# Unnormalized keys and queries in a gated-delta-rule layer: where the norm factors are applied

## The chip, the cores and the metric

The kernel runs on one core of one Trainium2 chip. The metric is device time of one execution, in microseconds (us); lower is better. A core has five instruction streams: TensorE (PE in the profile, with its weight loads as PEld), VectorE (DVE), ScalarE (ACT), GpSimd (POOL) and SyncE (SP). Here SP issues nearly all DMA transfers, one after another in program order. An instruction that waits holds up all that stands behind it on its own stream.

## The reference

One transformer block on 256 tokens of width 2048, all in float32: a norm, an input projection, two mixers of eight heads each (a gated delta rule, "GDN", and a causal attention, "MOBA"), an output projection, and a mixture of 32 experts of width 512, two for each token. The change lies in the GDN heads:

```python
qh = l2norm(heads(q)) * (HEAD_DIM ** -0.5)      # x * rsqrt(sum(x*x) + 1e-6), per token and head
kh = l2norm(heads(k))
...
kb = k * beta[..., None]
L = jnp.where(strict, jnp.einsum('bhnid,bhnjd->bhnij', kb, k) * decay, 0.0)
rhs = jnp.concatenate([v * beta[..., None], kb * jnp.exp(g)[..., None]], axis=-1)
sol = lax.linalg.triangular_solve(eye + L, rhs, left_side=True, lower=True)
attn = jnp.where(causal, jnp.einsum('bhnid,bhnjd->bhnij', q, k) * decay, 0.0)
...
o = rmsnorm(o, out_norm_w) * jax.nn.silu(zf)
```

A norm factor is one number for each token and head, so it may be multiplied in before or after the products over the head dimension.

## The kernel before

**Projection stage.** The two projections are cut into 18 chunks of 512 output columns, and each chunk into 16 units of 128 rows of the weight, 288 units in all. The chunks come in this order (half 0 is heads 0 to 3, half 1 heads 4 to 7): gk0, gq0, gv0, gz0, mv0, gk1, gq1, gv1, mk0, mq0, mk1, gz1, mq1, mv1, wo0 to wo3. Chunk gz0 is thus units 48 to 63. A unit's float32 weight tile `w_raw` is loaded by SP, split by ACT into a rounded `w_hi` (line 210) and by DVE into the rest `w_lo` (line 213), and multiplied by PE in 12 matmuls (lines 232 to 236) or, in the gz, mv and wo chunks, in 6 of twice the width (lines 243 to 246), always into the tile `pj`. Loads are written up to eight units ahead (`RAWB = 4` tiles of two units), splits five units ahead of PE (`SPB = 6`).

**Tasks.** Everything else of the mixers is written as Python generators that a loop steps once for each unit (`tick`, at most three of them in a unit). The number that a `yield` gives is the wait in units, 2 if none. What a task issues in the step of unit n lies behind unit n's matmuls on PE, but behind the split of a later unit on ACT and DVE, and behind a later load on SP. This order is fixed when the program is built. A second list, `side`, is stepped twice in a unit and holds the triangular inverse (`inverse`), a long run of small DVE instructions.

**The GDN steps that the change touches**, for each half:

- `decay` loads, for each of four heads, rows of cumulated decay, broadcast over all partitions, from a DRAM tensor `drow` into a tile `E` (128x6x128): one load of slots 0 to 3 (line 396) and one of slots 4 and 5 (line 398), whose rows are those of slots 1 and 3 once more. Then POOL masks slots 0, 2, 4 and 5 (`affine_select`, line 405), and ACT takes exponentials of all six (lines 410 to 412).
- `qk_task` runs for k and then for q: a convolution and silu (`conv_silu`), squares, and column sums of the squares on PE (`pss`, line 463). After q, DVE adds epsilon (lines 469, 470), POOL raises 16 columns to the power -1/2 (`rk`, line 472), PE transposes them (`prk`, line 475), ACT copies them out (line 477), SP stores them to DRAM (line 480) and loads them broadcast as `RN`, 256 KB for each head (line 484), and POOL multiplies keys and queries by them (line 487, four `kq` multiplications of 128x512). Then for each head PE forms the products (`pA`, lines 493 and 498), DVE multiplies them by `E` (lines 495, 499), and SP stores part of `E` to DRAM as `dU` for the inverse.
- `v_task` transposes v (`pv`) and scales it by `beta` on its way out of PSUM (`bv`, line 570).
- `head_task` finishes the inverse, applies it, and forms the output `po`, its mean square (line 648), the root (lines 650, 651) and the gated output `og` (line 653).

PSUM tiles of all tasks come from one ring of four buffers (`ps_tmp`).

**Expert stage.** From unit 225 on, loads of expert weights are put between the loads of `w_out` into buffers that are free, and from the end of the projections on the kernel streams some 400 MB of expert weights through them (SP, line 940), each load waiting for PE to be done with a buffer.

Of the kernel before, what the change touches and what calls it, by code (L numbers as in the profile page):

```python
# [19 lines left out]
T = 256  # L20
# [27 lines left out]
def tile_block(ctx, tc, x, norm_mix_w, w_in, conv_w, A_log, dt_bias, gonw, monw, w_out, nfw,  # L48
# [28 lines left out]
    def ps_tmp(name):  # L77
        return pp.tile([128, 512], F32, name=name, tag="pt", bufs=4)
# [19 lines left out]
    nc.vector.memset(mhalf, -0.5)  # L98
    ones1 = prc.tile([128, 1], F32, name="ones1")
# [287 lines left out]
    E = {}  # L387

    def decay(hf):

        heads = range(4 * hf, 4 * hf + 4)
        for H in heads:
            e = wt("E", [128, 6, 128], "E", EB)
            E[H] = e
            off = drow.offset + H * 256
            nc.sync.dma_start(e[:, 0:4].rearrange("p (a b) t -> p a (b t)", a=2),
                              bass.AP(tensor=drow.tensor, offset=off, ap=[[0, 128], [2048, 2], [1, 256]]))
            nc.sync.dma_start(e[:, 4:6],
                              bass.AP(tensor=drow.tensor, offset=off + 128, ap=[[0, 128], [2048, 2], [1, 128]]))
            yield 1  # L400
        yield 1
        for H in heads:
            e = E[H]
            for s, op in ((0, OP.is_gt), (2, OP.is_ge), (4, OP.is_gt), (5, OP.is_ge)):
                nc.gpsimd.affine_select(out=e[:, s], in_=e[:, s], pattern=[[1, 128]], compare_op=op, fill=-BIG, base=0,
                                        channel_multiplier=-1)
            yield 1
        for H in heads:
            e = E[H]
            nc.scalar.activation(e[:, 0:4:2], e[:, 0:4:2], AF.Exp, bias=negG[:, 0, H:H + 1])  # L410
            nc.scalar.activation(e[:, 1:4:2], e[:, 1:4:2], AF.Exp, bias=suf[:, H:H + 1])
            nc.scalar.activation(e[:, 4:6], e[:, 4:6], AF.Exp, bias=negG[:, 1, H:H + 1])
            if H % 2:
                yield 1
# [24 lines left out]
    kq, bv, zs, pss, YY = {}, {}, {}, {}, {}  # L439

    def qk_task(hf, la, pb):
# [25 lines left out]
        rk = wt("rk", [128, 4, 2, 2], "rk", 1)  # L467
        psv = pss[hf][:, 0:16].rearrange("p (h a b) -> p h a b", h=4, a=2)
        nc.vector.tensor_scalar(rk[:, :, 0], psv[:, :, 0], EPS, None, op0=OP.add)
        nc.vector.tensor_scalar(rk[:, :, 1], psv[:, :, 1], EPS, float(HD), op0=OP.add, op1=OP.mult)  # L470
        rkf = rk.rearrange("p h a b -> p (h a b)")
        nc.gpsimd.tensor_tensor(rkf, rkf, mhalf, op=OP.pow)
        yield 4
        prk = ps_tmp("prk")
        nc.tensor.transpose(prk[:16, 0:128], rkf, ident)
        rks = wt("rks", [16, 128], "rks", 1)
        nc.scalar.copy(rks, prk[:16, 0:128])
        yield
        drk = drp.tile([16, 128], F32, name=f"drk{hf}")
        nc.sync.dma_start(drk, rks)  # L480
        yield
        RN = [wt("RN", [128, 2, T], "YY", 4) for _ in range(4)]
        for h in range(4):
            nc.sync.dma_start(RN[h].rearrange("p a t -> p (a t)"), bcast_rows(drk, h * 512, 512))
        yield
        for h in range(4):
            nc.gpsimd.tensor_mul(kq[4 * hf + h], kq[4 * hf + h], RN[h])
            yield 1
        for h in range(4):
            H = 4 * hf + h  # L490
            e = E[H]
            p0 = ps_tmp("pA0")
            nc.tensor.matmul(p0, kq[H][:, 0, 0:128], kq[H].rearrange("p a t -> p (a t)"), start=True, stop=True)
            e0 = e[:, 0:4].rearrange("p s t -> p (s t)")
            nc.vector.tensor_mul(e0, p0, e0)
            p1 = ps_tmp("pA1")
            p1v = p1[:, 0:256].rearrange("p (a t) -> p a t", a=2)
            nc.tensor.matmul(p1v, kq[H][:, 0, 128:256], kq[H][:, :, 128:256], start=True, stop=True)
            nc.vector.tensor_mul(e[:, 4:6], p1v, e[:, 4:6])
            yield 1  # L500
            nc.sync.dma_start(square(dU[hf], h), e[:, 0:5:4])
        yield
# [12 lines left out]
    def inverse(hf):  # L515
# [10 lines left out]
        for j in range(30, -1, -1):  # L526
            n = 32 - j
            pr = wt("ybp", [128, 8, 32], "ybp", 1)[:, :, 0:n]
            nc.vector.tensor_tensor(pr, UB[:, j, None, j:32].to_broadcast([128, 8, n]), YB[:, :, j:32], op=OP.mult)
            yield  # L530
            nc.vector.tensor_reduce(YB[:, :, j:j + 1], pr, axis=AX.X, op=OP.add, negate=True)
            yield
# [21 lines left out]
    def v_task(hf, pb):  # L554
# [7 lines left out]
        yield 1  # L562
        for h in range(4):
# [5 lines left out]
            for b in range(2):  # L569
                nc.scalar.activation(bv[H][:, b], pv[:, b * 128:(b + 1) * 128], AF.Copy, scale=beta[:, b, H:H + 1])  # L570
# [21 lines left out]
    def head_task(H):  # L592
# [53 lines left out]
        so = wt("so", [128, 2], "so", 6)  # L646
        for b in range(2):
            nc.scalar.activation(og[:, b], po[:, b * 128:(b + 1) * 128], AF.Square, accum_out=so[:, b:b + 1])
# [3 lines left out]
        yield 1  # L652
        for b in range(2):
# [804 lines left out]
```

## Time and profile before

| | |
|---|---|
| time, median of 3 runs (lowest to highest) | 1455.63 us (1455.09 to 1456.22) |
| the profiled execution: its time / its span | 1455.25 us / 1453.5 us |
| busy in the span: PE, DVE, ACT, POOL | 1392.8, 621.2, 414.4, 58.9 us |
| mean granted TensorE clock | 0.991 |
| bytes moved by DMA | 493.4 MB |

The span is from the first to the last instruction; 1.75 us of the time lie outside it. PE counts as busy nearly always, but its matmuls overlap, so a late operand shows partly as an idle gap and partly as a matmul that starts later than its predecessor would allow. In the projection stage the starts of units are therefore the better measure of pace. Starts are us from the span's start throughout.

### The profile page before, as it was taken

The numbers are of one execution on the slowest core, as the hardware profiler recorded it, in microseconds if no ns is written. First come the engines' busy times: TensorE is split into PE (matmuls) and PEld (weight loads), VectorE is DVE, ScalarE is ACT, GpSimd is POOL, SyncE is SP. The second block draws the span as 40 slices with busy tenths as digits, with TensorE's granted clock in tenths as the row PEclk, the third lists the DMA queues.
The fourth block names the chain that finished last, engine by engine and source line by source line (L and its number), as shares of the span: only waits on it lengthen the run. The fifth ranks groups of instructions, "written<-read, shape, count | busy, mean of one in ns | idle before, by whom it ended". The sixth has DMA issues, their size and how long they took to land.

```text
span 1453.5 us, 19069 instructions
## 1 busy us (share of the span) xinstructions
PE 1392.8 (96%) x7490; PEld 817.5 (56%) x7490; DVE 621.2 (43%) x1289; ACT 414.4 (29%) x803; POOL 58.9 (4%) x92
## 2 busy tenths in 40 slices
PE   8989999999999999999999999999999999899996
PEld 8976999898988853443443443443443344235332
DVE  6856977497665442331331341251142033125024
ACT  5554544555554421120120120121121012013012
POOL 2021003200000000000000000000000000000010
PEclk9999999999999999999999999999999999999998
DMA  8656755766489579999999999999999999999996
GB/s 248 173 161 183 209 163 146 208 186 176 138 323 404 178 309 425 425 422 427 424 415 426 428 424 424 425 424 427 426 425 425 424 424 428 426 425 425 425 391 213
DMA packets 110224, 493.40 MB, mean 339 GB/s; under 512 B 23073, under 2 KB 33409, under 8 KB 81329
## 3 DMA queue, kind: packets, MB, share of 16 engines
q1 hardware_dynamic: 109392, 491.14, 87.0%
q8 instruction: 61, 1.00, 0.3%
q10 hardware_dynamic: 432, 0.79, 0.1%
q0 software_dynamic: 304, 0.20, 0.1%
q14 instruction: 35, 0.28, 0.1%
HBM read 488.12 MB, written 3.97 MB: 339 GB/s over the span
## 4 chain that ended last, share of the span: by engine, by line
PE 77%; DMA 13%; DVE 5%; ACT 3%; issue 1%; SPq 0%; ACTq 0%; POOL 0%; DVEq 0%
PE py L1335 15%; PE pgate L1070 12%; PE pup L1070 11%; DMA we<-in_w_expert_up_dram 5%; PE pj L232 5%; PE pj L233 5%; PE pj L236 5%; PE pj L246 4%; PE pj L243 4%; PE pj L244 3%; PE pcm L1322 3%; DMA we<-in_w_expert_down_dram 3%; PE ph L1059 3%; DVE acc L1324 2%; DMA we<-in_w_expert_gate_dram 2%; ACT xh L1004 1%
## 5 line engine op out<-in xcount | busy, mean ns | idle before, releaser
L213 DVE TENSOR_TENSOR w_lo<-w_raw,w_hi 128x512 fp32r<-128x512 f32 x288 | 195.1, 693 | 117.2 <-ACT w_hi L210 114.4
L210 ACT CAST w_hi<-w_raw 128x512 fp32r<-128x512 f32 x288 | 170.4, 619 | 110.1 <-DMA w_raw<-in_w_in_dram 53.1
L1070 PE MATMUL pup<-we,hT 128*64 128x512 f32 x608 | 165.6, 606 | 7.8 <-DMA we<-in_w_expert_up_dram 7.8
L232 PE MATMUL pj<-xth,w_hi 128*128 128x256 f32 x640 | 168.6, 296 | 0.0
L233 PE MATMUL pj<-xtl,w_hi 128*128 128x256 f32 x640 | 161.4, 284 | 0.0
L1070 PE MATMUL pgate<-we,hT 128*64 128x512 f32 x528 | 148.4, 595 | 0.0
L1335 PE MATMUL py<-we,hgT 128*64 128x512 f32 x480 | 144.8, 597 | 1.1 <-ACT hgT L1303 0.7
L232 PEld LDWEIGHTS pj<-xth,w_hi 128*128 128x128 f32 x640 | 123.3, 193 | 1.9 <-ACT w_hi L210 0.4
L233 PEld LDWEIGHTS pj<-xtl,w_hi 128*128 128x128 f32 x640 | 123.4, 193 | 0.2
L1048 DVE TENSOR_TENSOR hT<-ph,nfe 128x512 f32<-128x512 f32 x64 | 44.0, 688 | 169.2 <-PE pup L1070 131.9
L1296 DVE SCALAR_TENSOR_TENSOR hg<-pup,sl,hg 128x512 f32<-128x512 f32 x16 | 12.0, 750 | 232.4 <-PE pup L1070 224.5
L1070 PEld LDWEIGHTS pup<-we,hT 128*64 128x64 f32 x608 | 51.9, 139 | 100.5 <-issue 89.0
L1313 DVE SCALAR_TENSOR_TENSOR yl<-py,sl,yh 128x512 fp32r<-128x512 f32 x56 | 40.3, 746 | 158.3 <-ACT yh L1312 157.3
L1312 ACT ACTIVATE yh<-py,sl 128x512 fp32r<-128x512 f32 x56 | 37.6, 687 | 238.6 <-PE py L1335 212.4
L236 PE MATMUL pj<-xth,w_lo 128*128 128x256 f32 x640 | 103.5, 284 | 0.0
L1004 ACT CAST xh<-xs 128x512 fp32r<-128x512 f32 x64 | 73.8, 1187 | 93.9 <-PE ph L1059 62.0
L1005 DVE TENSOR_TENSOR xl<-xs,xh 128x512 fp32r<-128x512 f32 x64 | 70.4, 1116 | 52.6 <-PE ph L1059 34.9
L1070 PEld LDWEIGHTS pgate<-we,hT 128*64 128x64 f32 x528 | 46.1, 137 | 78.1 <-issue 75.3
L236 PEld LDWEIGHTS pj<-xth,w_lo 128*128 128x128 f32 x640 | 89.1, 193 | 0.0
L1324 DVE TENSOR_TENSOR acc<-acc,pcm 128x512 f32<-128x512 f32 (+1 forms) x122 | 75.3, 673 | 22.0 <-PE pcm L1322 22.0
L1335 PEld LDWEIGHTS py<-we,hgT 128*64 128x64 f32 x480 | 45.8, 136 | 67.2 <-issue 64.5
L1070 PE MATMUL pgate<-wm,hT 128*64 128x512 f32 x256 | 81.1, 595 | 0.0
(337 smaller groups left out, 2005.7 us busy)
## 6 DMA issues: line engine op xcount, KB each, us to landing
we<-in_w_expert_up_dram SPq DMA_DIRECT2D x38, 2048.0 KB, 25.8
we<-in_w_expert_gate_dram SPq DMA_DIRECT2D x33, 2048.0 KB, 22.9
we<-in_w_expert_down_dram SPq DMA_DIRECT2D x30, 2048.0 KB, 29.1
w_raw<-in_w_in_dram SPq DMA_DIRECT2D x111, 512.0 KB, 4.3
wm<-in_w_expert_gate_dram SPq DMA_DIRECT2D x16, 2048.0 KB, 28.1
wx<-in_w_expert_gate_dram SPq DMA_DIRECT2D x28, 1024.0 KB, 24.5
wx<-in_w_expert_down_dram SPq DMA_DIRECT2D x28, 1024.0 KB, 29.5
wx<-in_w_expert_up_dram SPq DMA_DIRECT2D x28, 1024.0 KB, 25.8
```

Of the source, the lines that this page charges most:

```text
L210: nc.scalar.copy(hi, raws[n])
L213: nc.vector.tensor_sub(lo, raws.pop(n), hi.bitcast(F32))
L232: nc.tensor.matmul(o, wh[:, cs], xh[k], start=(k == 0 and c % 2 == 0), stop=False, skip_group_check=True)
L233: nc.tensor.matmul(o, wh[:, cs], xl[k], start=False, stop=False, skip_group_check=True)
L236: nc.tensor.matmul(o, wl[:, cs], xh[k], start=False, stop=(k == NK - 1), skip_group_check=True)
L243: nc.tensor.matmul(pb[b], ah[:, bs], wh, start=(k == 0), stop=False)
L246: nc.tensor.matmul(pb[b], ah[:, b * 128:(b + 1) * 128], wl, start=False, stop=(k == NK - 1))
L1004: nc.scalar.copy(hi, src)
L1005: engine.tensor_sub(lo, src, hi.bitcast(F32))
L1070: nc.tensor.matmul(pgu[j * SL:(j + 1) * SL], hT[:, i, c0:c0 + SL], ws[j][kk], start=(half + kk == 0), stop=(half == 1 and kk == 7))
L1324: nc.vector.tensor_add(acc(b, c0, n), acc(b, c0, n) if g + pr else xs[:, b, c0:c0 + n], pc[:, 0:n])
L1335: nc.tensor.matmul(py[c][j * SL:(j + 1) * SL], hgT[pr][:, f, j * SL:(j + 1) * SL], ws[j][f % 2 * 4 + c], start=(f == 0), stop=(f == 3))
```

## The change

Keys and queries are left unnormalized. The squared-norm factors are used in three places instead. For each half, `rk2` holds 1/(sum of squares of k + eps), and DVE multiplies it in as a per-partition scalar where it multiplied the products by `E` already (`scalar_tensor_tensor` for `tensor_mul`). `bq` holds two roots: the first, of k's sum, with a power of +1/2, is multiplied by beta and takes beta's place as the scale of `bv`; the second, for q, is the scale of the output's square and is multiplied into the factor of the gated output. The transpose, the copy, the store, the four `RN` loads and the four POOL multiplications of each half are gone. Slots 4 and 5 of `E` are not loaded; POOL's `affine_select` reads slots 1 and 3 and writes 4 and 5. The remaining load of a head is written every two units instead of every unit. The products `pA` are written six units earlier in half 0 and at the same units as before in half 1, and only once that head's exponentials have been written. The `dU` stores are written two steps behind their products, and the store of the finished inverse three units later.

```diff
     def decay(hf):
@@ for H in heads: (loads)
-            nc.sync.dma_start(e[:, 4:6],
-                              bass.AP(tensor=drow.tensor, offset=off + 128, ap=[[0, 128], [2048, 2], [1, 128]]))
-            yield 1
+            yield 2
         yield 1
@@ for H in heads: (masks)
-            for s, op in ((0, OP.is_gt), (2, OP.is_ge), (4, OP.is_gt), (5, OP.is_ge)):
-                nc.gpsimd.affine_select(out=e[:, s], in_=e[:, s], pattern=[[1, 128]], compare_op=op, fill=-BIG, base=0,
+            for s, r, op in ((0, 0, OP.is_gt), (2, 2, OP.is_ge), (4, 1, OP.is_gt), (5, 3, OP.is_ge)):
+                nc.gpsimd.affine_select(out=e[:, s], in_=e[:, r], pattern=[[1, 128]], compare_op=op, fill=-BIG, base=0,
                                         channel_multiplier=-1)
@@ def qk_task, after the sums of q
-        rk = wt("rk", [128, 4, 2, 2], "rk", 1)
-        psv = pss[hf][:, 0:16].rearrange("p (h a b) -> p h a b", h=4, a=2)
-        nc.vector.tensor_scalar(rk[:, :, 0], psv[:, :, 0], EPS, None, op0=OP.add)
-        nc.vector.tensor_scalar(rk[:, :, 1], psv[:, :, 1], EPS, float(HD), op0=OP.add, op1=OP.mult)
-        rkf = rk.rearrange("p h a b -> p (h a b)")
-        nc.gpsimd.tensor_tensor(rkf, rkf, mhalf, op=OP.pow)
+        rk = wt("rk", [128, 2, 4, 2], "rk", 1)
+        psv = pss[hf][:, 0:16].rearrange("p (h a b) -> p a h b", h=4, a=2)
+        nc.vector.tensor_scalar(rk[:, 0], psv[:, 0], EPS, None, op0=OP.add)
+        nc.vector.tensor_scalar(rk[:, 1], psv[:, 1], EPS, float(HD), op0=OP.add, op1=OP.mult)
+        nc.vector.reciprocal(rk2[hf], rk[:, 0])
+        nc.gpsimd.tensor_tensor(bq[hf].rearrange("p a h b -> p a (h b)"), rk.rearrange("p a h b -> p a (h b)"), halves_,
+                                op=OP.pow)
         yield 4
-        prk = ps_tmp("prk")
-        nc.tensor.transpose(prk[:16, 0:128], rkf, ident)
-        rks = wt("rks", [16, 128], "rks", 1)
-        nc.scalar.copy(rks, prk[:16, 0:128])
-        yield
-        drk = drp.tile([16, 128], F32, name=f"drk{hf}")
-        nc.sync.dma_start(drk, rks)
-        yield
-        RN = [wt("RN", [128, 2, T], "YY", 4) for _ in range(4)]
-        for h in range(4):
-            nc.sync.dma_start(RN[h].rearrange("p a t -> p (a t)"), bcast_rows(drk, h * 512, 512))
-        yield
-        for h in range(4):
-            nc.gpsimd.tensor_mul(kq[4 * hf + h], kq[4 * hf + h], RN[h])
+        nc.vector.tensor_mul(bq[hf][:, 0], bq[hf][:, 0], beta[:, :, 4 * hf:4 * hf + 4].rearrange("p b h -> p h b"))
+        scaled.add(hf)
+        yield 1
+        for h in range(6):
+            if h < 4:
+                H = 4 * hf + h
+                while H not in decayed:
+                    yield 1
...
+                nc.vector.scalar_tensor_tensor(e0, p0, rk2[hf][:, h, 0:1], e0, op0=OP.mult, op1=OP.mult)
...
+                nc.vector.scalar_tensor_tensor(e[:, 4:6], p1v, rk2[hf][:, h, 1:2], e[:, 4:6], op0=OP.mult, op1=OP.mult)
+            if h >= 2:
+                nc.sync.dma_start(square(dU[hf], h - 2), E[4 * hf + h - 2][:, 0:5:4])
             yield 1
@@ def inverse, before the store of YB
+        for _ in range(6):
+            yield
@@ def v_task
-                nc.scalar.activation(bv[H][:, b], pv[:, b * 128:(b + 1) * 128], AF.Copy, scale=beta[:, b, H:H + 1])
+                nc.scalar.activation(bv[H][:, b], pv[:, b * 128:(b + 1) * 128], AF.Copy, scale=bq[hf][:, 0, h, b:b + 1])
@@ def head_task
+            nc.scalar.activation(og[:, b], po[:, b * 128:(b + 1) * 128], AF.Square, scale=rq[:, b:b + 1],
+                                 accum_out=so[:, b:b + 1])
...
+        nc.vector.tensor_mul(so, so, rq)
```

Three places in the built order show what moved. Rows are in program order of one engine; xN is N alike in a row; line numbers are those of each version's own file. The first place is SP in chunk gz0, where the decay rows of half 0 are loaded between the weights. Before:

```order
L205 DMA w_raw<-in_w_in_dram 128x2x512
L396 DMA E<-drow 128x2x256
L398 DMA E<-drow 128x2x128
L205 DMA w_raw<-in_w_in_dram 128x2x512
L396 DMA E<-drow 128x2x256
L398 DMA E<-drow 128x2x128
L396 DMA E<-drow 128x2x256
L398 DMA E<-drow 128x2x128
L205 DMA w_raw<-in_w_in_dram 128x2x512
L396 DMA E<-drow 128x2x256
L398 DMA E<-drow 128x2x128
L205 DMA w_raw<-in_w_in_dram 128x2x512 x4
```

The same place of the change:

```order
L208 DMA w_raw<-in_w_in_dram 128x2x512
L399 DMA E<-drow 128x2x256
L208 DMA w_raw<-in_w_in_dram 128x2x512
L399 DMA E<-drow 128x2x256
L208 DMA w_raw<-in_w_in_dram 128x2x512
L399 DMA E<-drow 128x2x256
L208 DMA w_raw<-in_w_in_dram 128x2x512
L399 DMA E<-drow 128x2x256
L208 DMA w_raw<-in_w_in_dram 128x2x512 x5
```

Between two weight loads there stood two to four `E` loads, and now there is one; the fourth head's comes one weight load later.

The second place is the whole of POOL's work for both halves. Before (`so` is the root in `head_task`):

```order
L405 AFFINE_SELECT E<-E 128x128 x4
L472 TENSOR_TENSOR rk<-rk,mhalf 128x16
L405 AFFINE_SELECT E<-E 128x128 x12
L487 TENSOR_TENSOR kq<-kq,RN 128x512 x4
L651 TENSOR_TENSOR so<-so,mhalf 128x2 x4
```

Of the change:

```order
L478 TENSOR_TENSOR bq_149<-rk,halves 128x16
L406 AFFINE_SELECT E<-E 128x128 x16
L655 TENSOR_TENSOR so<-so,mhalf 128x2 x4
L478 TENSOR_TENSOR bq_150<-rk,halves 128x16
L406 AFFINE_SELECT E<-E 128x128 x16
```

The multiplications are gone, and in half 0 the root now stands ahead of all sixteen masks.

The third place is ACT at the end of chunk mk0 and the beginning of mq0, with `bv` and the exponentials of half 1. Before:

```order
L570 ACTIVATE bv<-pv,beta 128x128 x2
L410 ACT_TABLE_LOAD
L410 ACTIVATE E<-E,negG 128x2x128
L411 ACTIVATE E<-E,suf 128x2x128
...
L210 CAST w_hi<-w_raw 128x512
L570 ACTIVATE bv<-pv,beta 128x128 x2
L410 ACTIVATE E<-E,negG 128x2x128
L411 ACTIVATE E<-E,suf 128x2x128
...
L210 CAST w_hi<-w_raw 128x512
L570 ACTIVATE bv<-pv,beta 128x128 x2
```

Of the change:

```order
L572 ACTIVATE bv<-pv,bq_150 128x128 x2
L213 CAST w_hi<-w_raw 128x512
L572 ACTIVATE bv<-pv,bq_150 128x128 x2
L213 CAST w_hi<-w_raw 128x512
L572 ACTIVATE bv<-pv,bq_150 128x128 x2
L411 ACT_TABLE_LOAD
L411 ACTIVATE E<-E,negG 128x2x128
L412 ACTIVATE E<-E,suf 128x2x128
```

All four heads' `bv` now stand ahead of the table load and the exponentials; before, three of the four stood behind six or twelve of them.

## Rows read from the trace of the kernel before

**Rows 1.** Windows, matmuls of `pj` alone: window and length, PE busy (count), then others.

```profile
90.62:109.32 18.70, 12.68 (x51) 8.55 (x50) 1.53 (x4) 0.00 (x0) 1.00 0.52 165
109.32:132.28 22.96, 13.74 (x49) 8.45 (x48) 1.53 (x4) 1.14 (x2) 0.93 0.60 177
132.28:154.25 21.97, 21.97 (x96) 18.19 (x97) 0.00 (x0) 0.15 (x2) 1.00 0.86 223
```

**Rows 2.** Timeline of PE in gz0: start us, length us, instruction.

```profile
126.81 0.48 PE L243 MATMUL pj<-w_hi,xth 128*128 128x512 f32 x1
...
129.71 0.48 PE L243 MATMUL pj<-w_hi,xth 128*128 128x512 f32 x1
```

**Rows 3.** Waits of PE over the whole run: us in total, times, longest us.

```profile
PE pj L246 <- DVE w_lo L213: 3.6, 3, 3.1
PE pj L243 <- ACT w_hi L210: 3.1, 3, 1.4
...
PE prk L475 <- POOL rk L472: 2.6, 1, 2.6
...
PE pA L493 <- ACT bv L570: 1.4, 1, 1.4
...
PE pA L498 <- ACT bv L570: 0.6, 1, 0.6
```

**Rows 4.** Windows, all work: PE, PEld, DVE, ACT, POOL busy, clock, DMA share, GB/s.

```profile
476.00:500.00 24.00, 24.00 (x119) 20.00 (x118) 12.59 (x20) 10.77 (x22) 0.00 (x0) 1.00 0.45 139
...
600.00:1000.00 400.00, 390.79 (x1750) 160.04 (x1748) 119.87 (x180) 65.47 (x80) 0.00 (x0) 1.00 1.01 424
```

**Rows 5.** Timeline of SP's queue around gz0: start us, us until the last issue.

```profile
85.89 2.44 SPq L398 DMA_DIRECT2D E<-drow  x1
88.42 7.01 SPq L205 DMA_DIRECT2D w_raw<-in_w_in_dram  x4
```

**Rows 6.** DMA issues of the whole run: count, KB each, median us to landing.

```profile
w_raw<-in_w_in_dram SPq DMA_DIRECT2D x111, 512.0 KB, 4.3
...
E<-drow SPq DMA_DIRECT2D x8, 256.0 KB, 9.7
...
E<-drow SPq DMA_DIRECT2D x8, 128.0 KB, 9.9
```

**Rows 7.** Timeline of ACT in gz0; idle time before it in brackets.

```profile
92.95 1.14 ACT L210 CAST w_hi<-w_raw 128x512 fp32r<-128x512 f32 x2 [6.81 <-DMA w_raw<-in_w_in_dram]
```

**Rows 8.** Timeline of POOL in gz0.

```profile
97.77 3.45 POOL L405 TENSOR_SCALAR_AFFINE_SELECT E<-E 128x128 f32<-128x128 f32 x12
111.80 6.08 POOL L487 TENSOR_TENSOR kq<-kq,RN 128x512 f32<-128x512 f32 x4 [10.58 <-DMA RN<-drk]
```

**Rows 9.** Timeline of DVE in gz0.

```profile
99.89 0.69 DVE L213 TENSOR_TENSOR w_lo<-w_raw,w_hi 128x512 fp32r<-128x512 f32 x1 [4.85 <-ACT w_hi L210]
...
105.34 2.45 DVE L432 SCALAR_TENSOR_TENSOR cc<-cc,colw 128x255 f32<-128x255 f32 x6
...
115.25 4.48 DVE L432 SCALAR_TENSOR_TENSOR cc<-cc,colw 128x255 f32<-128x255 f32 x6
```

**Rows 10.** Windows as in 4, two stretches in which the granted clock fell.

```profile
120.30:123.00 2.70, 2.60 (x4) 1.50 (x5) 2.54 (x5) 1.95 (x5) 0.00 (x0) 0.50 0.33 61
202.10:205.50 3.40, 3.40 (x35) 3.11 (x34) 2.06 (x7) 1.24 (x6) 0.00 (x0) 0.50 0.30 70
```

**Rows 11.** Timeline of ACT at the end of mk0.

```profile
260.84 1.28 ACT L410 ACT_TABLE_LOAD   x1
262.14 0.51 ACT L410 ACTIVATE E<-E,negG 128x256 f32<-128x256 f32 x1
```

**Rows 12.** Groups by line: count, busy us, mean ns of one, idle before.

```profile
L472 POOL TENSOR_TENSOR rk<-rk,mhalf 128x16 f32<-128x16 f32 x2 | 6.5, 3248 | 14.9 <-DVE rk L470 14.9
...
L1296 DVE SCALAR_TENSOR_TENSOR hg<-pup,sl,hg 128x512 f32<-128x512 f32 x16 | 12.0, 750 | 232.4 <-PE pup L1070 224.5 <-ACT hg L1295 7.9
...
L495 DVE TENSOR_TENSOR E<-pA,E 128x512 f32<-128x512 f32 x8 | 5.5, 689 | 1.6 <-PE pA L493 1.6
```

More of the change, by code (lines that the diff above doesn't have):

```diff
@@ L98, in tile_block @@
     nc.vector.memset(mhalf, -0.5)
+    halves_ = prc.tile([128, 2, 8], F32, name="halves")
+    nc.vector.memset(halves_[:, 0], 0.5)
+    nc.vector.memset(halves_[:, 1], -0.5)
     ones1 = prc.tile([128, 1], F32, name="ones1")
@@ L385, in decay_task @@
         push(decay(0), 3)
-    E = {}
+    E, decayed = {}, set()
     def decay(hf):
@@ L412, in decay @@
             nc.scalar.activation(e[:, 4:6], e[:, 4:6], AF.Exp, bias=negG[:, 1, H:H + 1])
+            decayed.add(H)
             if H % 2:
@@ L437, in conv_silu @@
             yield 1
-    kq, bv, zs, pss, YY = {}, {}, {}, {}, {}
+    kq, bv, zs, pss, YY, scaled = {}, {}, {}, {}, {}, set()
+    rk2 = [prc.tile([128, 4, 2], F32, name=f"rk2{hf}") for hf in range(2)]
+    bq = [prc.tile([128, 2, 4, 2], F32, name=f"bq{hf}") for hf in range(2)]
     def qk_task(hf, la, pb):
@@ L489, in qk_task @@
[L489 to L501, printed above, removed]
@@ L502, in qk_task @@
-        yield
+        rk = wt("rk", [128, 2, 4, 2], "rk", 1)
[5 more added lines that the diff above has]
+                                op=OP.pow)
@@ new lines, in qk_task @@
+        yield 4
+        nc.vector.tensor_mul(bq[hf][:, 0], bq[hf][:, 0], beta[:, :, 4 * hf:4 * hf + 4].rearrange("p b h -> p h b"))
[6 more added lines that the diff above has]
+                    yield 1
+                e = E[H]
+                p0 = ps_tmp("pA0")
+                nc.tensor.matmul(p0, kq[H][:, 0, 0:128], kq[H].rearrange("p a t -> p (a t)"), start=True, stop=True)
+                e0 = e[:, 0:4].rearrange("p s t -> p (s t)")
+                nc.vector.scalar_tensor_tensor(e0, p0, rk2[hf][:, h, 0:1], e0, op0=OP.mult, op1=OP.mult)
+                p1 = ps_tmp("pA1")
+                p1v = p1[:, 0:256].rearrange("p (a t) -> p a t", a=2)
+                nc.tensor.matmul(p1v, kq[H][:, 0, 128:256], kq[H][:, :, 128:256], start=True, stop=True)
+                nc.vector.scalar_tensor_tensor(e[:, 4:6], p1v, rk2[hf][:, h, 1:2], e[:, 4:6], op0=OP.mult, op1=OP.mult)
+            if h >= 2:
+                nc.sync.dma_start(square(dU[hf], h - 2), E[4 * hf + h - 2][:, 0:5:4])
+            yield 1
@@ L503, in qk_task @@
+        yield 2
         side.append(inverse(hf))
@@ L562, in v_task @@
         yield 1
+        assert hf in scaled
         for h in range(4):
@@ L646, in head_task @@
         so = wt("so", [128, 2], "so", 6)
+        rq = bq[H // 4][:, 1, H % 4]
         for b in range(2):
-            nc.scalar.activation(og[:, b], po[:, b * 128:(b + 1) * 128], AF.Square, accum_out=so[:, b:b + 1])
+            nc.scalar.activation(og[:, b], po[:, b * 128:(b + 1) * 128], AF.Square, scale=rq[:, b:b + 1],
+                                 accum_out=so[:, b:b + 1])
         yield 1
```

## Prediction

> **What bounds the kernel now.** I began with the late stage, to learn what a microsecond saved earlier is worth. There are two windows to read. Through the expert stage the DMA engines are busy all the time (share 1.01 at 424 GB/s from 600 to 1000 us), while PE is busy 390.8 of 400 us: the stream of weights sets the pace and PE is close behind. But from 476 to 500 us, with the projections still running, the DMA share is only 0.45 [rows 4]. The prefetch has filled every free buffer by then and waits for PE. So the expert stage begins, at the end of the projections, with full buffers, and its length does not depend on when that is. Whatever shortens the projection stage shortens the run by as much, until the 24 us of slack are used up.
>
> The projection stage is paced by PE as long as weights come in time. The measure is the chunk: mv0, 16 units of the 6-matmul kind, takes 21.97 us, or 1.373 us a unit. Chunk gz0, of the same kind, takes 18.70 us for its first eight units and 22.96 us for the other eight [rows 1]. It has more PE work than mv0 only by the products `pA` and the transposes `pv` of half 0, in its last four units: the starts at 126.81 and 129.71 are one such unit, 2.90 us, or 1.53 us over a bare one [rows 2]; four of them are 6.1 us. So gz0 loses 18.70 - 8 x 1.373 = 7.7 us in its first half and 22.96 - 8 x 1.373 - 6.1 = 5.9 us in its second. PE's list of waits names the causes: `w_hi` and `w_lo` late, the transpose `prk` late because of POOL's root, and, in half 1, `pA` waiting for `bv` [rows 3].
>
> **First half of gz0: 7.7 us.** `prk` waits 2.6 us for POOL's root [rows 3]; the change has no transpose there, so this goes for certain. The other 5.1 us are weights that come late. While the decay rows of half 0 are loaded, single issues hold SP for 2.44 us, and the four weight loads behind them go out over 7.0 us [rows 5]. ACT then stands idle for 6.81 us until a weight tile lands [rows 7]. An `E` load of 128 KB takes as long to land as one of 256 KB, 9.9 and 9.7 us, and a weight load of 512 KB only 4.3 [rows 6]: here the number of small pieces counts and not the bytes, since both kinds of `E` load have two pieces for each of 128 partitions. The change takes away half of the `E` loads, hence half of the pieces, and writes the rest one between two weight loads where there were two to four. No row shows loads spaced like that. From below, nothing but the `prk` wait goes (2.6 us); from above, all of it (7.7 us). I take 6.7 us, near the upper end, because a quarter as many pieces go in between two weight loads at the worst place (one load for four); the 1 us is left for the four loads that stay.
>
> **Second half of gz0: 5.9 us.** Here POOL multiplies `kq` by `RN` for 6.08 us [rows 8]. In that time six convolution steps of DVE take 4.48 us; the same six took 2.45 us ten microseconds earlier [rows 9]. `w_lo` comes late, and PE has its longest wait, 3.1 us [rows 3]. Then the granted clock falls to 0.50, so from 2.4 to 1.2 GHz, in 120.30 to 123.00 us, in which PE runs 2.6 us of work [rows 10]; the wait and about 1.3 us for that slow stretch, with the smaller gaps, make up the 5.9. The multiplications are gone, so I take 5.9 us. From below it is the wait by name, 3.1 us, if the clock falls anyway.
>
> **Half 1: 2.0 us.** There `pA` waits 1.4 + 0.6 us for a PSUM buffer that `bv` still has to empty [rows 3], because ACT has a table load of 1.28 us and exponentials of 0.51 us in between [rows 11]. The change puts all `bv` ahead of them. I take 2.0; the bounds are 0, if the products then wait for the exponentials instead, and 2.0. The late weights that also occur here cost PE nothing that its list of waits shows.
>
> **What is added.** DVE's products become three-operand instructions: 750 ns against 689 for 128x512 [rows 12], so 8 x 0.06 = 0.5 us, and as much at most for the smaller ones, all on DVE, which has 0.69 us of splitting [rows 9] in a unit of 1.37. The reciprocal, the product with beta and eight products with `rq` are instructions on a few columns, a few tenths of a microsecond each at most. They hide behind the five units by which splits are ahead. New waits need a closer look. The product with beta waits for POOL's root (3.25 us, rows 12), and is written four units, 5.5 us, behind it: nothing. In half 0 the products now come right behind the exponentials: a table load and twelve exponentials, 1.28 + 12 x 0.51 = 7.4 us [rows 11], during which only one `w_hi` gets through on ACT. DVE's products and the `w_lo` behind them wait as well. Against that stand five units of split weights and four units' products, 5 x 1.37 + 6.1 = 13 us of PE work: nothing. The upper bound is the 3.1 us that `w_hi` kept PE waiting in all [rows 3]. Half 1's inverse and heads move four to five units later, beside the attention task of half 1; PE's work is the same, 0 to 1 us, and I take 0. The two memsets at the start lie beside the load of x.
>
> **The sum.** 6.7 + 5.9 + 2.0 = 14.6 us off 1455.25 us is 1440.65 us; the median of the runs is 0.4 us above that execution, so 1441 us. By the lower bounds with the new wait it would be 2.6 + 3.1 + 0 - 3.1 - 1 = 1.6 us, all ends bad at once; by the upper ones 15.6. A second stretch at half clock, at 202.10 us [rows 10], follows a row of very small matmuls and not a wait; the change shifts those by one unit, and 3.4 us at half clock are worth 1.7 us, either way.
>
> **A rule against it.** In the change all sixteen masks of half 0 run in one piece, at 0.29 us each [rows 8], 4.6 us, while DVE has weights to split. In the old trace a `w_lo` that begins inside a run of twelve masks takes 0.69 us, no more than elsewhere [rows 9], so I add nothing. The Trainium skill, "SBUF — State Buffer" (its part on which operations take the port shared by VectorE and GpSimd), says that a VectorE instruction with two SBUF inputs and a GpSimd instruction that reads SBUF exclude each other for the whole instruction; `w_lo` and the masks are such instructions. By that rule DVE would stand still for up to 4.6 us a half, and the sum would be 5.4 us instead of 14.6; the row at 99.89 us does not bear it out for masks, though the stretched convolution beside the `kq` multiplications does for those.
>
> **Rivals.** (1) The decay loads hold SP's queue as before, being still there: only the `prk` wait goes in the first half, 2.6 + 5.9 + 2.0 = 10.5, 1445 us. For it: no row shows the spaced loads. Against it: half the pieces. (2) The masks in one piece stop DVE, and its slack of five units is not enough: 2 x 4.6 us are lost, 1450 us. Against it stands the `w_lo` of 0.69 us. (3) Nothing reaches the end, because the weight stream alone decides: 1455.6 us. For it: share 1.01 through the stage. Against it: share 0.45 before the stage. (4) Slower: the exponentials wait for late decay rows, and the weight splits behind them on ACT stop PE. The last head's rows are loaded one weight load, 2.7 us, later. If SP were as late as now, at 88.3 us, they would be issued at 91 and land 9.7 us later at 101 us; the exponentials of the last two heads are written for about 100 us. That is 1 to 2 us of waiting, and the cover is 13 - 7.4 = 5.6 us. Only when the rows land over 5.6 + 14.6 = 20 us late does it decide: 30 us for a load, three times what any has shown; then 1460 us or more.
>
> **How the numbers follow.** A measurement of this kernel tells 0.2%, 2.9 us, from no change. The forecast, 1436 to 1445 us, has 0.67, rival (1) with its surroundings (1445 to 1448) 0.15, (2) 0.05, (3) 0.06, (4) and whatever else makes it slower 0.04, and a gain beyond the forecast, below 1436, 0.03. The range from 1436 to 1448 leaves out (2), (3), (4) and the greater gain, 0.18. Faster is 0.67 + 0.15 + 0.05 + 0.03 = 0.90, the same 0.06, slower 0.04.
>
> **What would show it.** Chunk gz0 should take about 29 us instead of 41.66, with no idle time before `w_hi` or `w_lo` of over a microsecond. Weight loads beside the `E` loads should be issued without issues of 2 us before them. DVE's convolution steps should take 2.45 us for six throughout gz0, and the clock should not fall at its end. `pA` of half 1 should not wait for `bv`. The stage from 600 us on should look the same and begin some 14 us earlier, with the DMA share still below 0.6 ahead of it. The prediction is wrong if PE waits for `pA`'s PSUM buffers or for `w_hi` behind the exponentials, or if the prefetch is no longer full when the projections end.

## The result and the profile after

The changed kernel takes 1440.53 us (median of 5 runs, 1440.20 to 1441.84) against 1455.63 us, a ratio of 0.990 with a 95% interval of 0.9889 to 0.9911. The forecast was 1441 us. The profiled execution is the slowest of the five: 1441.84 us, span 1440.1 us.

The windows of `pj` show chunk gz0 in its two halves and mv0 (as in [rows 1]), and mk0 with mq0, first of the change, then, for the last, of the kernel before. The columns are window and length, PE, PEld, DVE and ACT busy, clock, DMA share, GB/s.

```profile
90.54:104.45 13.91, 12.03 (x52) 9.37 (x51) 3.05 (x8) 0.00 (x0) 1.00 0.43 120
104.45:118.56 14.11, 12.23 (x48) 8.38 (x47) 0.00 (x0) 0.03 (x1) 1.00 0.66 168
118.56:140.34 21.78, 21.78 (x98) 18.02 (x96) 0.00 (x0) 1.26 (x3) 1.00 0.94 255
...
224.06:278.18 54.12, 48.81 (x385) 47.02 (x385) 4.55 (x12) 0.00 (x0) 1.00 0.74 190
```

```profile
237.78:294.89 57.11, 48.90 (x386) 47.06 (x386) 4.54 (x12) 0.00 (x0) 1.00 0.71 196
```

So gz0 went from 41.66 to 28.02 us (13.6 gained; the terms said 12.6) and half 1's chunks from 57.11 to 54.12 (3.0; the term said 2.0). A bare gz0 is 16 x 1.36 = 21.8 us and 6.1 us of products and transposes: nothing is left to gain there.

SP's queue at the place of [rows 5] issues each decay load in under half a microsecond, and the transfers land sooner than in [rows 6]:

```profile
73.64 0.42 SPq L399 DMA_DIRECT2D E<-drow  x1
75.76 0.37 SPq L208 DMA_DIRECT2D w_raw<-in_w_in_dram  x1
76.18 0.46 SPq L399 DMA_DIRECT2D E<-drow  x1
...
83.60 9.62 SPq L208 DMA_DIRECT2D w_raw<-in_w_in_dram  x4
```

```profile
w_raw<-in_w_in_dram SPq DMA_DIRECT2D x111, 512.0 KB, 4.1
E<-drow SPq DMA_DIRECT2D x8, 256.0 KB, 6.0
```

The four weight loads at 83.60 take 9.62 us to go out because they now wait for free buffers: weights are ahead, where in [rows 5] they were behind (from 60 to 100 us SP waits 22.8 us for `w_lo` to free a buffer, before 9.9 us). PE's list of waits holds none of the five entries of [rows 3]; its longest are of the expert stage and the start:

```profile
PE ph L1064 <- DVE xl L1010: 8.4, 13, 1.8
PE pup L1075 <- DMA we<-in_w_expert_up_dram: 7.8, 4, 3.8
...
PE px L183 <- DMA xs<-in_x_dram: 3.2, 2, 1.9
```

Windows over all work: the DMA share is low ahead of the end of the projections (493.1 us) and 1.01 behind it, as in [rows 4]. The first line is the one stretch of the projection stage at half clock.

```profile
188.60:192.10 3.50, 3.50 (x29) 3.09 (x28) 1.80 (x5) 1.06 (x4) 0.00 (x0) 0.51 0.17 20
460.00:485.00 25.00, 25.00 (x124) 20.81 (x123) 13.38 (x22) 11.44 (x24) 0.00 (x0) 1.00 0.51 165
600.00:1000.00 400.00, 390.44 (x1754) 159.84 (x1752) 116.50 (x180) 63.35 (x78) 0.00 (x0) 1.00 1.01 424
```

The last projection matmul starts 15.2 us earlier (493.1 against 508.3), and from there to the end of the span it is 947.0 us against 945.3.

### The profile page after: what moved, and what is told of

It reads as the page before. It is cut to its first block, busy times and chain, and to the rows that moved or that the text cites. A ratio compares the mean times of both kernels' runs of the same rounds, so it can differ in the third digit from the quotient of the medians.

```text
span 1440.1 us, 19014 instructions
## 1 busy us (share of the span) xinstructions
PE 1387.6 (96%) x7488; PEld 813.1 (56%) x7488; DVE 620.0 (43%) x1303; ACT 416.6 (29%) x801; POOL 49.7 (3%) x84
## 4 chain that ended last, share of the span: by engine, by line
PE 76%; DMA 14%; DVE 5%; ACT 3%; issue 1%; SPq 0%; ACTq 0%; POOL 0%; DVEq 0%
PE py L1340 15%; PE pgate L1075 12%; PE pup L1075 12%; PE pj L235 6%; PE pj L239 5%; PE pj L236 5%; DMA we<-in_w_expert_up_dram 4%; PE pcm L1327 3%; DMA we<-in_w_expert_down_dram 3%; PE pj L246 3%; PE pj L247 3%; PE pj L249 3%; PE ph L1064 3%; DMA wm<-in_w_expert_up_dram 2%; DVE acc L1329 2%; DMA w_raw<-in_w_out_dram 2%
```

## Experiments

The forecast held, but as a sum of separate causes: late weights (4.1 us), the wait of `prk` (2.6), POOL's multiplications (5.9), the order of `bv` (2.0). That is **theory P**. The rival, **theory S**, has one cause: the decay loads make the weights late, this empties the stock of five units of splits that lies ready ahead of PE, and the other waits are consequences. In the trace of before DVE shows why `prk` had to wait: the epsilon instructions of `rk`, on which POOL's root hangs, stood behind a `w_lo` that came 6.74 us late. The timeline of DVE:

```profile
93.60 0.69 DVE L213 TENSOR_TENSOR w_lo<-w_raw,w_hi 128x512 fp32r<-128x512 f32 x1 [6.74 <-ACT w_hi L210]
94.21 0.16 DVE L469 TENSOR_SCALAR rk<-pss 128x8 f32<-128x8 f32 x1
```

**loads_only.** The kernel before, with the loads of the change alone.

```diff
-            nc.sync.dma_start(e[:, 4:6],
-                              bass.AP(tensor=drow.tensor, offset=off + 128, ap=[[0, 128], [2048, 2], [1, 128]]))
-            yield 1
+            yield 1 if hf else 2
...
-            for s, op in ((0, OP.is_gt), (2, OP.is_ge), (4, OP.is_gt), (5, OP.is_ge)):
-                nc.gpsimd.affine_select(out=e[:, s], in_=e[:, s], pattern=[[1, 128]], compare_op=op, fill=-BIG, base=0,
+            for s, r, op in ((0, 0, OP.is_gt), (2, 2, OP.is_ge), (4, 1, OP.is_gt), (5, 3, OP.is_ge)):
+                nc.gpsimd.affine_select(out=e[:, s], in_=e[:, r], pattern=[[1, 128]], compare_op=op, fill=-BIG, base=0,
```

> The kernel before with one part of the change: slots 4 and 5 of E are not loaded but masked out of slots 1 and 3, and in half 0 the loads that stay are written two units apart (half 1: one unit apart). The transpose prk, its copy, the RN loads, the four kq multiplications on POOL and the order of bv stay as before. Theory P (each part has its own term, as in the prediction): only the late weights go, 4.1 us of the first half of gz0; prk still waits 2.6 us for POOL's root and the multiplications still cost 5.9 us: 1455.6 - 4.1 = 1451.5 us. Theory S (one stock: the late weights drain the five units of splits, the root is late because DVE's rk stands behind a w_lo that waits for them, and POOL's multiplications cost only because the stock is empty): the whole loss of gz0 goes, 12 to 13.6 us, so 1442 to 1444 us, with no wait of prk over 0.5 us and no half clock at 120 us although POOL multiplies kq as before.

Measured: 1442.72 us (1440.55 to 1445.91), ratio 0.991 (0.9894 to 0.9926). The windows of `pj` (gz0; mk0 with mq0) and the one wait of gz0 that is left, with DVE's timeline ahead of it:

```profile
90.75:121.07 30.32, 23.45 (x99) 17.42 (x97) 3.05 (x8) 1.14 (x2) 1.00 0.59 180
225.18:279.93 54.75, 48.89 (x385) 47.05 (x385) 4.59 (x12) 0.00 (x0) 1.00 0.72 201
```

```profile
PE pj L246 <- DVE w_lo L213: 2.1, 1, 2.1
```

```profile
105.55 4.50 DVE L430 SCALAR_TENSOR_TENSOR cc<-cc,colw 128x255 f32<-128x255 f32 x6
109.98 3.31 DVE L213 TENSOR_TENSOR w_lo<-w_raw,w_hi 128x512 fp32r<-128x512 f32 x5
```

Of 13.6 us in gz0 the loads alone bring 11.3, of 3.0 in half 1 2.4. P's 1451.5 us is refuted. The waits for `prk` and, in half 1, for `bv` are gone although their instructions stand as before. What is left, 2.3 us, is a `w_lo` behind convolution steps that take 4.50 us beside the `kq` multiplications.

**old_loads.** The change with the two old loads for each head, one unit apart, and the old masks.

```diff
+            nc.sync.dma_start(e[:, 4:6],
+                              bass.AP(tensor=drow.tensor, offset=off + 128, ap=[[0, 128], [2048, 2], [1, 128]]))
-            yield 2
+            yield 1
...
```

> The change with the old decay loads put back in both halves: both loads for each head, one unit apart, masks reading their own slots. Everything else as in the change. Theory P: the 4.1 us of late weights come back, 1440.5 + 4.1 = 1444.6 us; no prk and no kq multiplication are there to add anything. Theory S: the late weights alone are the disease, so at least the 7.7 us of the first half of gz0 come back, and the products right behind the exponentials find no stock: 1448 to 1454 us. A rival on the decay loads (they cost nothing, the rest of the change brought it all): 1440 to 1441 us.

Measured: 1452.38 us (1451.52 to 1456.22), ratio to the kernel before 0.9968 (0.9957 to 0.9979): most of the gain is gone. The windows of `pj` (gz0; mk0 with mq0) in the profiled run, which took 1456.22 us:

```profile
90.53:128.57 38.04, 24.77 (x99) 17.75 (x97) 3.06 (x8) 0.04 (x1) 0.96 0.64 169
234.37:293.92 59.55, 49.45 (x387) 47.98 (x385) 4.59 (x13) 0.00 (x0) 0.97 0.68 191
```

The timelines of ACT, DVE and PE:

```profile
93.42 1.14 ACT L213 CAST w_hi<-w_raw 128x512 fp32r<-128x512 f32 x2 [7.43 <-DMA w_raw<-in_w_in_dram]
99.88 1.14 ACT L213 CAST w_hi<-w_raw 128x512 fp32r<-128x512 f32 x2 [5.33 <-DMA w_raw<-in_w_in_dram]
101.04 1.28 ACT L413 ACT_TABLE_LOAD   x1
```

```profile
105.38 0.69 DVE L216 TENSOR_TENSOR w_lo<-w_raw,w_hi 128x512 fp32r<-128x512 f32 x1 [1.94 <-ACT w_hi L213]
...
106.07 2.45 DVE L436 SCALAR_TENSOR_TENSOR cc<-cc,colw 128x255 f32<-128x255 f32 x6
...
109.03 0.75 DVE L495 SCALAR_TENSOR_TENSOR E<-pA,rk,E 128x512 f32<-128x512 f32 x1
```

```profile
100.55 0.50 PE L246 MATMUL pj<-w_hi,xth 128*128 128x512 f32 x1 [2.13 <-ACT w_hi L213]
109.83 2.07 PE L493 MATMUL pA<-kq 128*128 128x512 f32 x2 [4.96 <-DVE E L495]
```

ACT works in order: behind the late `w_hi` stand the exponentials of two heads, and behind these the next `w_hi`. Its `w_lo` on DVE comes 1.94 us late, six convolution steps follow, and only then the product that empties a PSUM buffer. PE waits for that buffer with its third `pA`. This is the mechanism of rival (4), with late weights in the place of late decay rows.

**prk_back.** The change with the transpose and its copy put back (nothing reads the copy).

```diff
         yield 4
+        prk = ps_tmp("prk")
+        nc.tensor.transpose(prk[:16, 0:128], bq[hf].rearrange("p a h b -> p (a h b)"), ident)
+        rks = wt("rks", [16, 128], "rks", 1)
+        nc.scalar.copy(rks, prk[:16, 0:128])
```

> The change with the transpose prk of POOL's roots and its copy by ACT put back in each half, four units behind the root as before; nothing reads the copy. Theory P: the transpose waits for POOL's root, 2.6 us in half 0: 1443.1 us. Theory S: the root was late in the old kernel only because DVE's rk stood behind weights that had not come; with weights in time the transpose finds the root done, PE shows no wait for it, and the time is 1440.5 to 1441 us (0.3 us for a transpose and 0.25 us of ACT a half).

Measured: 1440.34 us (1439.62 to 1442.24), PE has no wait for it; gz0 takes 28.18 us. In loads_only, where the transpose stands as before, it didn't wait either. The 2.6 us were a consequence of the late weights.

**pool_mults and mults_beside_taps.** The change with four POOL multiplications of 128x512 added in each half, ahead of the products, and behind the second head's product.

```diff
+                nc.gpsimd.tensor_mul(wt("RN", [128, 2, T], "YY", 4), kq[H], kq[H])
                 p0 = ps_tmp("pA0")
```

```diff
+            if h == 1:
+                for _ in range(4):
+                    nc.gpsimd.tensor_mul(wt("RN", [128, 2, T], "YY", 4), kq[H],
+                                         e[:, 0:4].rearrange("p (a b) t -> p a (b t)", a=2))
             if h >= 2:
```

> The change with four POOL multiplications of 128x512 put back in each half, one ahead of each head's product pA, into a scratch tile that nothing reads. They touch no result; PE does not wait for them. Theory P: they slow DVE's convolutions as before and cost 5.9 us in half 0 (3.1 at least): 1443.6 to 1446.4 us. Theory S: with the stock of splits full they cost nothing, 1440.5 to 1441 us, although each takes about 1.5 us on POOL and stretches what DVE does beside it.

> The change with four POOL multiplications of 128x512 added in each half, all behind the second head's product (they read it, so that they start when it is done), into a scratch tile that nothing reads. In half 0 they then lie beside the six convolution steps and the w_lo that follow, which they did not do when put ahead of the products. Theory P: the steps take 4.5 us instead of 2.45, w_lo is late, and gz0 loses 3.1 to 5.9 us: 1443.6 to 1446.4 us. Theory S: DVE is stretched as much, but five units of splits cover 2 to 4 us: gz0 stays at 28 to 28.5 us.

Measured: 1444.52 us (1439.43 to 1445.11) and 1443.85 us (1440.57 to 1449.48). The times alone would speak for P, but the time is not where P has it. In the first, gz0 is as in the change and the loss lies in a longer stretch at half clock, 85 us later; the windows of `pj` in gz0, and of all work there:

```profile
91.13:119.16 28.03, 24.27 (x99) 17.75 (x97) 3.05 (x8) 0.04 (x1) 1.00 0.55 147
```

```profile
190.05:200.29 10.24, 10.24 (x74) 9.09 (x73) 5.10 (x14) 3.03 (x8) 0.00 (x0) 0.50 0.24 60
```

In the second they lie beside the six steps. DVE's, POOL's and PE's timelines:

```profile
106.35 6.55 DVE L434 SCALAR_TENSOR_TENSOR cc<-cc,colw 128x255 f32<-128x255 f32 x6
...
106.19 5.65 POOL L500 TENSOR_TENSOR RN<-kq,E 128x512 f32<-128x512 f32 x4 [6.28 <-DVE E L493]
...
114.22 0.44 PE L574 MATMUL pv<-ident,vT 128*128 128x128 f32 x2 [1.75 <-DVE E L493]
```

The steps take 6.55 us instead of the 2.44 to 2.45 that they take without POOL beside them, and gz0 30.01 us. So S too was off: a full stock leaves 2.0 us of the cost. PE loses it here to a `pv` whose buffer a DVE product frees late, in loads_only (2.3 us) to a `w_lo`. Either is well below the 5.9 us of the forecast and its lower bound of 3.1.

**mults_half1.** The same multiplications as in pool_mults in half 1 alone.

```diff
+                if hf:
+                    nc.gpsimd.tensor_mul(wt("RN", [128, 2, T], "YY", 4), kq[H], kq[H])
```

> The change with a POOL multiplication of 128x512 ahead of each product, in half 1 alone. With them in both halves the run took 4 us more, though gz0 took the same 28.03 us; the time lay in gv1, where the granted clock stayed at 0.50 for 10.2 us instead of 3.4, 80 us behind the multiplications of half 0 and 35 us ahead of those of half 1. If that stretch has nothing to do with the multiplications, it can appear here too, with a time of 1440 to 1445 us, but gz0 and mk0 with mq0 stay at 28.0 and 54.1 us. If the multiplications of half 0 bring it about, it stays at 3.4 us here and the run at 1440.5 us. If those of half 1 cost something themselves, mk0 with mq0 takes over 55 us.

Measured: 1444.45 us (1443.22 to 1446.53). gz0 (28.03 us) and mk0 with mq0 (54.13 us) are those of the change, and the stretch is there, 6.8 us long, with no multiplication ahead of it in half 0:

```profile
188.91:195.73 6.82, 6.82 (x55) 6.07 (x53) 2.85 (x8) 1.90 (x5) 0.00 (x0) 0.50 0.29 79
```

So the stretch doesn't need the multiplications of half 0. Whether it is also why 4 of 5 runs of pool_mults and all 5 here lie above 1443 us, and none of the change, is not settled: one run of each has a profile.

**dense_single, spaced_double and split_pieces.** What about the loads counts? The change with half 0's loads one unit apart; with both loads of a head, and the old masks, two units apart; and with each remaining load cut in two of 128 KB.

```diff
-            yield 2
+            yield 2 if hf else 1
```

```diff
+            nc.sync.dma_start(e[:, 4:6],
+                              bass.AP(tensor=drow.tensor, offset=off + 128, ap=[[0, 128], [2048, 2], [1, 128]]))
             yield 2
...
```

```diff
-            nc.sync.dma_start(e[:, 0:4].rearrange("p (a b) t -> p a (b t)", a=2),
-                              bass.AP(tensor=drow.tensor, offset=off, ap=[[0, 128], [2048, 2], [1, 256]]))
+            for b in range(2):
+                nc.sync.dma_start(e[:, b:4:2],
+                                  bass.AP(tensor=drow.tensor, offset=off + 128 * b, ap=[[0, 128], [2048, 2], [1, 128]]))
```

> The change with the loads of half 0 one unit apart instead of two (one load for each head, slots 4 and 5 masked out of 1 and 3; half 1 as in the change). Between two weight loads there then stand one, two and one of them. What is told apart is whether the number of the loads or their spacing brought the weights in time. By the number (half the pieces are gone): gz0 stays at 28 to 29 us and the run at 1440 to 1442 us. By the spacing: weights come late again, gz0 takes 32 us or more and the run 1444 us or more, with a gap of ACT before w_hi of over 3 us.

> The change with both loads for each head put back (masks reading their own slots), but two units apart, so that two stand between any two weight loads and never four. By the number of pieces: as many as in the old kernel, so the weights are late again, gz0 takes 34 to 38 us and the run 1447 to 1453 us, as with the old loads. By the spacing: gz0 at 28 to 30 us, the run at 1440 to 1443 us.

> The change with each remaining decay load cut in two: slots 0 and 2 by one transfer, slots 1 and 3 by another, both written at the place of the one. The same 256 KB for each head, in the same places between the weight loads, but in twice as many pieces (512 of 512 B instead of 256 of 1 KB), which is the number of pieces and of issues of the old kernel with two thirds of its bytes. If the number of pieces or issues keeps the weights waiting, as the prediction had it, gz0 takes 33 to 34 us as with the spaced double loads and the run 1449 to 1453 us. If the bytes do, nothing changes: gz0 28 us, the run 1440 to 1442 us.

Measured: 1440.96 us (1440.12 to 1442.13), 1452.39 us (1450.72 to 1456.08) and 1441.45 us (1439.67 to 1446.62). Windows of `pj` in gz0, of the three in this order:

```profile
90.53:118.56 28.03, 24.27 (x98) 17.75 (x97) 3.05 (x8) 0.03 (x1) 1.00 0.64 155
```

```profile
90.90:124.70 33.80, 24.78 (x98) 17.59 (x97) 3.05 (x8) 0.00 (x0) 1.00 0.53 159
```

```profile
90.48:118.69 28.21, 24.28 (x98) 17.75 (x97) 3.05 (x8) 0.00 (x0) 1.00 0.52 154
```

One load for each head is harmless at either spacing, two at neither. With two, the spacing may still matter: the medians of spaced_double and old_loads are alike, but in their profiles (of runs of 1456.08 and 1456.22 us) gz0 takes 33.80 against 38.04 us. And the number of pieces and issues, on which the prediction argued, does not decide: split_pieces has as many as the old kernel, at the same spacing as spaced_double, and loses 0.2 us in gz0. Its second issue of a pair is held on SP as well (the pair at 76.14 us takes 2.45 us), at no cost. Its DMA issues:

```profile
E<-drow SPq DMA_DIRECT2D x16, 128.0 KB, 6.3
```

The same size of transfer, in the same number of pieces, landed in 9.9 us in the old kernel [rows 6]. The weight loads among them, from 70 to 90 us, took this long to land in split_pieces and then in spaced_double:

```profile
w_raw<-in_w_in_dram SPq DMA_DIRECT2D x6, 512.0 KB, 6.7
```

```profile
w_raw<-in_w_in_dram SPq DMA_DIRECT2D x6, 512.0 KB, 9.9
```

What the old loads have more is 128 KB for each head, 384 instead of 256, read from rows that the first load reads too. Whether the bytes or the second reading of these rows is dear stays open; no run separates them.

**masks_twice.** Each mask written twice.

```diff
+                nc.gpsimd.affine_select(out=e[:, s], in_=e[:, r], pattern=[[1, 128]], compare_op=op, fill=-BIG, base=0,
+                                        channel_multiplier=-1)
```

> The change with each of POOL's masks done twice (the second leaves what the first wrote), so that 32 instead of 16 stand in a piece in each half: in the change 16 take 6.82 us of POOL beside w_lo and convolution steps of DVE, of which six took 2.72 us there and 2.45 us elsewhere. If masks stop DVE as long as they run (rival 2 of the prediction), DVE loses up to 6.8 us more a half and PE has a wait for w_lo or for a buffer: 1443 us or more. If they hardly touch DVE, only the exponentials start later, by up to 6.8 us, and the splits behind them on ACT; the stock of five units covers that if nothing else takes from it, so gz0 at 28 to 30 us and the run at 1440.5 to 1442.5 us. The Trainium skill, "SBUF - State Buffer", has the two exclude each other for whole instructions; by that it would be the first.

Measured: 1441.17 us (1440.39 to 1442.11); gz0 takes 28.48 us, 0.5 more. Rival (2) is refuted. In the change the masks lie beside DVE's work so:

```profile
92.89 6.82 POOL L406 TENSOR_SCALAR_AFFINE_SELECT E<-E 128x128 f32<-128x128 f32 x16
...
93.53 2.72 DVE L434 SCALAR_TENSOR_TENSOR cc<-cc,colw 128x255 f32<-128x255 f32 x6
```

It is POOL that is held up (0.43 us a mask against 0.29 in [rows 8]); DVE's six steps lose 0.3 us. Single masks of masks_twice show beside what: a convolution step, a `w_lo`, and an instruction that reads PSUM. Below them is DVE's `w_lo` with masks beside it (0.72 us each) and without (0.62 us):

```profile
94.96 0.47 POOL L406 TENSOR_SCALAR_AFFINE_SELECT E<-E 128x128 f32<-128x128 f32 x1
...
96.94 0.74 POOL L406 TENSOR_SCALAR_AFFINE_SELECT E<-E 128x128 f32<-128x128 f32 x1
...
98.93 0.29 POOL L406 TENSOR_SCALAR_AFFINE_SELECT E<-E 128x128 f32<-128x128 f32 x1
```

```profile
96.06 2.16 DVE L216 TENSOR_TENSOR w_lo<-w_raw,w_hi 128x512 fp32r<-128x512 f32 x3
...
114.36 2.48 DVE L216 TENSOR_TENSOR w_lo<-w_raw,w_hi 128x512 fp32r<-128x512 f32 x4
```

**bv_between.** The change with half 1's loads one unit apart, so that exponentials come between the `bv`.

```diff
-            yield 2
+            yield 1 if hf else 2
```

> The change with the loads of half 1 one unit apart instead of two, so that half 1's exponentials come three units earlier, two heads' ahead of the first bv and two between the first and the second, where in the change all bv stand ahead of them. Theory P (the order on ACT was what kept pA waiting for bv in half 1, 2.0 us): pA or pv waits for bv again, mk0 with mq0 takes 55 to 56 us, the run 1441.5 to 1442.5 us. Theory S (bv was late only because weights were): 53.8 to 54.3 us, the run as the change.

Measured: 1443.39 us (1438.52 to 1443.63), but mk0 with mq0 takes 54.46 us, 0.3 more than in the change, and PE has no wait for `bv`. The rest of the difference is again the stretch at half clock (10.2 us in this profile).

**sums_spread.** An attempt at a better kernel: the row of very small matmuls ahead of that stretch spread over four units.

```diff
                                 start=(la == 0 and h == 0 and b == 0), stop=True, skip_group_check=True)
+            if hf and la == 0 and h < 3:
+                yield 1
```

> The change with one edit: the column sums of k's squares of half 1 (sixteen matmuls of one column, in one unit at the end of gq1, together with nineteen 32x32 matmuls of the heads of half 0) are written over four units, two heads' worth moved one and two units on. Nothing is left out. Behind that unit the granted clock was at 0.50 for 0, 3.4, 6.8 or 10.2 us in the profiles so far, worth 0 to 5 us, and the times of kernels that are alike in gz0 differ by about that. If the row of very small matmuls in one place brings the stretch about, it goes, and the run takes 1437 to 1440 us with little scatter. If it comes whatever PE's work there, it stays, and the run takes 1440 to 1445 us.

Measured: 1440.00 us (1439.58 to 1440.75), ratio 0.9889 (0.9872 to 0.9905). The clock in its windows of all work is 1.00 where the change has the stretch:

```profile
186.00:200.00 14.00, 14.00 (x164) 13.22 (x163) 9.20 (x24) 5.69 (x16) 0.00 (x0) 1.00 0.39 112
```

Its scatter is the smallest here, 1.2 us, but it is not measurably faster than the change; and the stretch was also missing in the profiles of loads_only, prk_back, masks_twice and split_pieces, without this edit. That the spreading prevents it is likely from the scatter, not shown.

## Why the prediction was right, and where it was not

**The sum** (14.6 forecast) was right: gz0 gave 13.6 and half 1 3.0; 1.1 were lost in wo0 to wo2, 0.4 in gz1 and 1.8 from the projections' end on. That makes 13.3 of the 13.4 us between the two profiled executions; the medians differ by 15.1. The 1.8 us can't be laid to the change: the same stage took between 945.4 and 947.4 us in the twelve experiments.

**First half of gz0** (6.7): the size held, a part of the cause did not. The `prk` wait "goes for certain", but it was no term of its own: with weights in time the transpose costs nothing (prk_back). The loads, taken at 4.1, are worth all of it: loads_only needs 11.1 us for its first eight units, where bare ones take 10.9.

**Why the loads cost so much** was wrong in its mechanism. The step "the number of small pieces counts and not the bytes" falls with split_pieces, and the credit for spacing with dense_single. Behind it, what is dear in the second load of a head stays open. The landing times of [rows 6] could not tell: both kinds of load were in flight together, so neither time belongs to one kind alone.

**Second half of gz0** (5.9): the step that laid it all to POOL's multiplications failed. Put back where they touch the convolution they cost 2.0 us, and 2.3 us are left in loads_only; the other 3.6 went with the loads, which had emptied the stock ten microseconds earlier. The half clock at its end was missing in loads_only too, with the multiplications still there.

**Half 1** (2.0, measured 3.0): mis-sized and mis-named. 2.4 came from the loads; the order of `bv` is worth 0.3 (bv_between). The sentence that late weights "cost PE nothing that its list of waits shows" was the error: the list named `bv`, which on ACT stood behind a `w_hi` that waited for weights. ACT's timeline in the kernel before:

```profile
255.24 1.14 ACT L210 CAST w_hi<-w_raw 128x512 fp32r<-128x512 f32 x2 [4.93 <-DMA w_raw<-in_w_in_dram]
...
259.16 1.14 ACT L210 CAST w_hi<-w_raw 128x512 fp32r<-128x512 f32 x2 [2.15 <-DMA w_raw<-in_w_in_dram]
260.20 0.62 ACT L570 ACTIVATE bv<-pv,beta 128x128 f32<-128x128 f32 x2
```

**Added work** (0) held: masks, products and new waits are all covered; the lower bounds of the sum were far off. Two of the signs that the prediction named did not come out, without reaching PE: DVE stood idle for 1.79 and 1.17 us ahead of two `w_lo` behind the exponentials (101.57 and 104.49 us), and six convolution steps took 2.72 us beside the masks. **Rivals**: (1) did not happen: in half 0 SP issued each load that stayed in under half a microsecond; (2) fell with masks_twice; (3) with the start of the expert stage; (4) is real as a mechanism (old_loads) but needs late weights. That the sum came out although half its terms were misattributed is owed to all parts being in the change at once, and in that the hit was luck; a forecast for loads_only by the same steps would have missed by 9 us.

## What to carry to other kernels

A list of waits names the last releaser, not the first cause: before waits are added up as separate terms, ask of each whether the releaser itself stood behind something late on its in-order engine. Waits that follow one another within the depth of a prefetch can be one stock running empty, and then one edit is worth all of them. A cost that vanishes when the stock is full (here a transpose, and most of four multiplications) is not to be credited to removing it.

## What the runs showed of the hardware

In these traces POOL's masks and multiplications take turns, one for one, with DVE's instructions that have both inputs in SBUF, and a pair takes little more than the longer of the two. In mults_beside_taps the multiplications start 1.3 to 1.4 us apart (one alone takes 1.29 us, in half 1 of loads_only), and each of the four steps beside them takes 1.4 to 1.5 us instead of 0.4: here DVE pays, and both are done 6.7 us after the first began. In masks_twice a mask of 0.29 us takes 0.47 us beside a step and 0.74 us beside a `w_lo`, while the `w_lo` loses 0.1 us: here POOL pays. Beside an instruction that reads PSUM a mask loses nothing. The Trainium skill, "SBUF — State Buffer" (section "SBUF: two separate sides"), has a VectorE instruction with two SBUF inputs and a GpSimd instruction that reads SBUF exclude each other for the whole instruction. The trace agrees that they hold each other up, for masks too, but a pair takes less than the two one after the other (0.72 us for a mask of 0.29 and a `w_lo` of 0.62).

A stretch at 1.2 GHz (granted clock 0.50) followed the same row of small matmuls (16 of one column and, in the change, 20 of 32x32) in some executions and not in others: 0, 3.4, 6.8 or 10.2 us long in the profiles. The 10.2 us took some 3 us more than the 3.4, from the start of gq1 to the end of gv1 (63.5 against 60.7 us), and 4.2 more than none (59.3 in prk_back and split_pieces). That is larger than some of the terms that were to be told apart; only the windows by chunk could tell them. It need not be all of the scatter: the runs of split_pieces lie up to 7.0 us apart.
